# Half the feed-forward steps: 86 of 264 weight pieces by seven block products in place of eight

## The chip, the cores and the metric

The kernel runs on one core of one Trainium2 chip, as one launch. The metric is the device time of that core in microseconds, the median of the runs. The core has a matrix engine (TensorE, PE in the rows, with its weight loads as PEld), a vector engine (VectorE, DVE), an activation engine (ScalarE, ACT), GpSimd (POOL) and a queue engine that issues the transfers (SyncE, SP). Each takes its instructions in a fixed order.

## The reference

One layer of a hybrid decoder over 256 tokens of width 2048, in float32. What matters here are its two half steps, which hold some three fifths of the weights:

```python
D_MODEL = 2048
SEQ = 256
D_FF = 5632

def swiglu(x, w_gu, w_down):
    g, u = jnp.split(x @ w_gu, 2, axis=-1)
    return (jax.nn.silu(g) * u) @ w_down
...
        h = h + 0.5 * swiglu(rmsnorm(h, ffn1_norm[i]), ffn1_w_gu[i], ffn1_w_down[i])
...
        h = h + 0.5 * swiglu(rmsnorm(h, ffn2_norm[i]), ffn2_w_gu[i], ffn2_w_down[i])
    return rmsnorm(h, final_norm)
```

Between the half steps stand one input projection with a gating group and a state-space scan, one output projection, and cross attention into 256 memory tokens.

## The kernel before

All weights stream through the core once. The unit of work is a **piece**: 256 rows of a weight matrix (two blocks of 128, `KP`) by 1024 columns (two halves of 512, `j`). For the gate-and-up projection the two halves are the gate columns and the matching up columns of one column group `c` of 512; there are 11 groups of 8 pieces in a half step (a *column* below). For the down projection they are two neighbouring groups of output columns; there, a pass over the hidden pieces is made for output columns 0 and 1 and another for 2 and 3. The hidden width is taken in two parts, groups 0 to 5 and 6 to 10, each followed by its two down passes. Both half steps together have 2 x 11 x 8 = 176 gate-and-up pieces and 88 down pieces, 264.

Products are made to float32 accuracy from two reduced-precision parts of each operand. `split` (L139) takes a raw piece from the `wraw` buffers and makes, for each block of 128 rows, a rounded high part on ScalarE (`whi`, L148) and the remainder on VectorE (`wlo`, L149). `to_operand` (L229) does the same for the tokens: four transposes by TensorE into one PSUM bank (L72), then high and low halves of the operand. In `proj_tok` (L161) each pair of a token block `t` (two of 128) and a row block `k` multiplies into two PSUM banks, one for each half of the columns, by six matmuls of 512 columns (L180 to L185): high by high, high by low and low by high for each half. A piece is therefore 24 matmuls. TensorE's order is the program's order; for ScalarE and VectorE a planner fixes the order ahead of time, so that each of them waits at its head even where something behind is ready.

After the last piece of a column `evac` (L305) makes the hidden values from PSUM: Silu on ScalarE (L307) and one product on VectorE (L308) for each token block. `operand_later` (L249) puts their transposes off by one `step` (L77), that is, behind the first piece of the next column; they are read out by L236 and L237. In a down pass `evac` of `add_proj` (L286) adds 0.5 times the result to the stream `h` (L291). `finish` (L758) makes the final norm; in the last pass the last two pieces are ordered by token block (`apart` 2), so that block 0 is ready early.

PSUM has eight banks: six in the pool `mm` for products, two in `tp` for everything else (`side`, L90). SBUF holds three raw pieces (`wraw`), four halves of high and of low parts (`wsp`) and 13 slots of 8 KB a partition (`big`) for operands. At the start `x` and the first three weight pieces are loaded in turns (L319 to L324), and the operands of blocks 1 to 3 of `x` are made after pieces 1, 3 and 5 (L336).

## Time and profile before

| | us |
|---|---|
| median of 3 runs | 2575.32 (2575.3 to 2578.29) |
| the profiled execution, whole | 2575.8 |
| its span from the first to the last instruction | 2573.9 |
| TensorE matmuls, busy | 2536.2 |
| VectorE, busy | 1376.7 |
| ScalarE, busy | 1160.0 |

Times in rows are microseconds from the start of the span unless they are marked ns. A row of a group gives the line, engine, operation, output and inputs, shapes and count, then the busy time of the group and the mean of one; after the second bar stands the idle time of the engine right before them and what ended it. In a row in order of time the first number is the start and the second the length; a bracket gives the idle time before it and its releaser. Matmul records overlap: a matmul's record is longer than the distance to the next one's start.

### The profile page before, as it was taken

How to read it: one execution, taken by the hardware profiler on the slowest of the kernel's cores; microseconds unless marked ns; L12 is line 12 of the kernel's file. 1: busy time of each engine (PE TensorE's matmuls, PEld its weight loads, DVE VectorE, ACT ScalarE, POOL GpSimd, SP SyncE). 2: the span in 40 equal slices, each digit the busy share in tenths (PEclk: the TensorE clock that was granted, in tenths of full speed). 3: DMA queues.
4: the chain of work that ended last, by engine and by line, in shares of the span. 5: the costliest groups of instructions: out<-in, count | busy, mean ns of one | idle time of the engine just before them, and what ended most of it. 6: DMA issues, size and time to landing. Idle time of an engine off the chain costs nothing.

```text
span 2573.9 us, 31721 instructions
## 1 busy us (share of the span) xinstructions
PE 2536.2 (99%) x12990; PEld 2166.1 (84%) x12990; DVE 1376.7 (53%) x1445; ACT 1160.0 (45%) x1389; POOL 20.3 (1%) x44
## 2 busy tenths in 40 slices
PE   7999999999999999999999999999999999999998
PEld 6888888888889988788888999988888888888886
DVE  4545444544557667655555555555554454445454
ACT  5444433444445455535544544444444443344443
POOL 0000000000000000000000000000000000000000
PEclk9999999999999999999999999999999999999999
DMA  6555555555654555545655655555555556656564
GB/s 222 190 191 185 195 190 191 192 188 188 196 168 165 181 173 191 190 153 183 194 186 189 213 181 164 164 179 168 191 185 193 184 192 195 193 186 199 188 196 135
DMA packets 190368, 476.74 MB, mean 185 GB/s; under 512 B 12576, under 2 KB 12736, under 8 KB 189456
## 3 DMA queue, kind: packets, MB, share of 16 engines
q1 hardware_dynamic: 188400, 465.87, 55.7%
q0 software_dynamic: 1680, 8.73, 1.0%
q8 instruction: 101, 1.65, 0.3%
q14 instruction: 43, 0.35, 0.0%
q10 hardware_dynamic: 144, 0.13, 0.0%
HBM read 472.57 MB, written 2.13 MB: 184 GB/s over the span
## 4 chain that ended last, share of the span: by engine, by line
PE 97%; DMA 1%; DVE 1%; issue 0%; ACT 0%; SPq 0%; DVEq 0%; POOLq 0%; POOL 0%; ACTq 0%
PE acc L69 93%; PE tpose L72 2%; PE yp L69 1%; PE logits L69 0%; PE o L69 0%; DMA raw<-in_w_gu 0%; DMA dec<-cum_rows 0%; PE mixed L69 0%; ACT whi L148 0%; DVE cacc L376 0%; DVE wlo L149 0%; PE dt L69 0%; PE st L69 0%; PE scores L69 0%; PE yo L69 0%
## 5 line engine op out<-in xcount | busy, mean ns | idle before, releaser
L149 DVE TENSOR_TENSOR wlo<-raw,whi 128x1024 fp32r<-128x1024 f32 x880 | 1076.3, 1225 | 1073.8 <-ACT whi L148 1068.6
L148 ACT CAST whi<-raw 128x1024 fp32r<-128x1024 f32 x880 | 925.0, 1052 | 1229.3 <-PE acc L69 1209.6
L69 PE MATMUL acc<-whi,xt_ffn 128*128 128x512 f32 x2816 | 880.1, 391 | 8.7 <-ACT whi L148 8.7
L69 PEld LDWEIGHTS acc<-whi,xt_ffn 128*128 128x128 f32 x2816 | 529.3, 188 | 118.5 <-ACT whi L148 9.1
L69 PE MATMUL acc<-wlo,xt_ffn 128*128 128x512 f32 x1408 | 548.9, 390 | 0.5 <-DVE wlo L149 0.5
L69 PE MATMUL acc<-whi,hid 128*128 128x512 f32 x1408 | 436.8, 390 | 0.0
L69 PEld LDWEIGHTS acc<-wlo,xt_ffn 128*128 128x128 f32 x1408 | 264.8, 188 | 54.8 <-DVE wlo L149 1.0
L69 PEld LDWEIGHTS acc<-whi,hid 128*128 128x128 f32 x1408 | 264.3, 188 | 54.7
L69 PE MATMUL acc<-wlo,hid 128*128 128x512 f32 x704 | 274.0, 389 | 0.0
L69 PE MATMUL acc<-whi,xt_mix 128*128 128x512 f32 x768 | 242.5, 393 | 0.0
L69 PE MATMUL acc<-xt_mix,whi 128*128 128x256 f32 x1024 | 187.3, 285 | 0.0
L69 PEld LDWEIGHTS acc<-whi,xt_mix 128*128 128x128 f32 x768 | 144.2, 188 | 30.3 <-ACT whi L148 0.5
L69 PEld LDWEIGHTS acc<-xt_mix,whi 128*128 128x128 f32 x1024 | 160.9, 193 | 0.3
L69 PEld LDWEIGHTS acc<-wlo,hid 128*128 128x128 f32 x704 | 132.2, 188 | 27.3
L69 PE MATMUL acc<-wlo,xt_mix 128*128 128x512 f32 x384 | 149.7, 390 | 0.0
L69 PE MATMUL acc<-xt_mix,wlo 128*128 128x256 f32 x512 | 145.5, 284 | 0.0
L69 PEld LDWEIGHTS acc<-xt_mix,wlo 128*128 128x128 f32 x512 | 98.9, 193 | 0.0
L69 PE MATMUL acc<-memt,whi 128*128 128x256 f32 x512 | 92.9, 284 | 0.0
L69 PE MATMUL acc<-xt_xa,whi 128*128 128x256 f32 x512 | 92.9, 284 | 0.0
L69 PEld LDWEIGHTS acc<-wlo,xt_mix 128*128 128x128 f32 x384 | 72.1, 188 | 15.4 <-issue 0.7
L69 PE MATMUL acc<-whi,at 128*128 128x512 f32 x256 | 80.3, 391 | 0.0
L69 PEld LDWEIGHTS acc<-xt_xa,whi 128*128 128x128 f32 x512 | 79.8, 192 | 0.1
(211 smaller groups left out, 1904.9 us busy)
## 6 DMA issues: line engine op xcount, KB each, us to landing
raw<-in_w_gu SPq DMA_DIRECT2D x346, 512.0 KB, 4.5
raw<-in_w_dn SPq DMA_DIRECT2D x88, 1024.0 KB, 5.6
raw<-in_w_in SPq DMA_DIRECT2D x80, 1024.0 KB, 5.1
raw<-in_w_out SPq DMA_DIRECT2D x32, 1024.0 KB, 5.8
raw<-in_w_kv SPq DMA_DIRECT2D x32, 1024.0 KB, 5.4
raw<-in_w_q SPq DMA_DIRECT2D x16, 1024.0 KB, 5.2
raw<-in_w_o SPq DMA_DIRECT2D x16, 1024.0 KB, 5.9
dec<-cum_rows POOLq DMA_DIRECT2D x4, 1024.0 KB, 5.9
```

The costliest lines, as they stand in the source:

```text
L69: return pe(nc.tensor.matmul(out, lhsT=lhsT, rhs=rhs, start=start, stop=stop))
L72: return pe(nc.tensor.transpose(out=out, in_=in_, identity=identity))
L148: nc.scalar.copy(out=hi, in_=raw[:, k])
L149: nc.vector.tensor_tensor(out=lo, in0=raw[:, k], in1=hi.bitcast(F32), op=ALU.subtract)
```

## The change

Seen as two by two blocks, a piece multiplies four token blocks A(t, k) with four weight blocks B(k, j) into four outputs C(t, j), in eight block products. The change makes 86 of the 264 pieces of the two half steps (marked S) by Strassen's method in Winograd's form, with seven products of sums; the other 178 (C) stay as they were.

- For an S piece `split_sums` makes four sums of the raw weight blocks in float32 on VectorE, then high and low parts of three raw blocks and of the four sums. `Pieces.add` makes three plain forms and four sums of the token blocks, and their parts. `proj_sum` multiplies seven times, three matmuls each.
- Four products (m1, m6, m5, m7) collect in four banks of their own over all S pieces of a column or pass, the three others and the fourth output block (c11) with the C pieces. After the last S piece `mid` combines the four on VectorE. After the last piece `evac` adds the result to the other four. All eight banks are now one pool, and between the first and the last S piece no put-off job runs (`shut`).
- A column has its kinds in `GU_KINDS` (three of eight S), a down pass in `DN_KINDS` (two of ten or three of twelve). The hidden width is split after five groups in place of six. In the first column the pieces come in the order `FIRST`.
- High and low parts are made for a whole piece by one instruction, with three and two buffers; the sums and their parts have one buffer each. `big` has 12 slots in place of 13. Small tensors of the middle stages move into the buffers of the sums, and the memory kept for descriptors shrinks to 4096.
- The last pass no longer joins its last two pieces.

```diff
     wraw = ctx.enter_context(tc.tile_pool(name="wraw", bufs=3))
-    wsp = ctx.enter_context(tc.tile_pool(name="wsp", bufs=4))
-    big = ctx.enter_context(tc.tile_pool(name="big", bufs=13))
+    whigh = ctx.enter_context(tc.tile_pool(name="whigh", bufs=3))
+    wlow = ctx.enter_context(tc.tile_pool(name="wlow", bufs=2))
+    wsum = ctx.enter_context(tc.tile_pool(name="wsum", bufs=1))
+    wshigh = ctx.enter_context(tc.tile_pool(name="wshigh", bufs=1))
+    wslow = ctx.enter_context(tc.tile_pool(name="wslow", bufs=1))
+    big = ctx.enter_context(tc.tile_pool(name="big", bufs=12))
...
-    mm = ctx.enter_context(tc.tile_pool(name="mm", bufs=6, space=PSUM))
-    tp = ctx.enter_context(tc.tile_pool(name="tp", bufs=2, space=PSUM))
+    mm = ctx.enter_context(tc.tile_pool(name="mm", bufs=8, space=PSUM))
...
-    def step(to=None):
+    def step(shut=False):
...
         for job in sorted(put_off, key=lambda j: j[:2]):
-            if job[0] <= steps[0] or to == "end":
+            if job[0] <= steps[0] and not shut:
                 put_off.remove(job)
                 job[2]()
...
     def side(name):
-        return tp.tile([P, NC], F32, name=name, tag="tp")
...
+    PLAIN = {(0, 0): 0, (0, 1): 1, (1, 0): 2, (1, 1): 3}
+    FOR_SUMS = {(0, 0): 0, (1, 0): 1, (1, 1): 2, (0, 1): 3}
+
+    def load(w, r0, cs, at, fine=False):
+        raw = wraw.tile([P, 2 * KP, NC], F32, name="raw")
+        rows = w[r0:r0 + KP * P, :]
+        if at is PLAIN and cs[1] == cs[0] + NC:
...
+        for j, c in enumerate(cs):
+            b, e = at[0, j], at[1, j]
+            src = rows[:, c:c + NC]
+            if e > b and not fine:
+                nc.sync.dma_start(out=raw[:, b:e + 1:e - b, :], in_=src.rearrange("(k p) n -> p k n", p=P))
+                continue
+            for k, x in enumerate((b, e)):
+                nc.sync.dma_start(out=raw[:, x, :], in_=src[k * P:(k + 1) * P, :])
         return raw
...
-    def split(raw, behind=()):
-
-        parts = []
-        for k in range(KP):
-            hi = wsp.tile([P, 2, NC], F32R, name="whi")
-            lo = wsp.tile([P, 2, NC], F32R, name="wlo")
-            with ExitStack() as order:
-                for ins in behind:
-                    order.enter_context(tc.issue_after(ins))
-                nc.scalar.copy(out=hi, in_=raw[:, k])
-                nc.vector.tensor_tensor(out=lo, in0=raw[:, k], in1=hi.bitcast(F32), op=ALU.subtract)
-            parts.append((hi, lo))
-        return parts
+    def high(pool, x, n):
+        t = pool.tile([P, 2 * KP, NC], F32R, name="hi")
+        nc.scalar.copy(out=t[:, :n], in_=x[:, :n])
+        return t
+
+    def low(pool, x, hi, n):
+        t = pool.tile([P, 2 * KP, NC], F32R, name="lo")
+        nc.vector.tensor_tensor(out=t[:, :n], in0=x[:, :n], in1=hi[:, :n].bitcast(F32), op=ALU.subtract)
+        return t
...
+    def split(raw):
+        hi = high(whigh, raw, 2 * KP)
+        return hi, low(wlow, raw, hi, 2 * KP)
...
+    def split_sums(raw):
+        t = wsum.tile([P, 4, NC], F32, name="sum")
+        nc.vector.tensor_tensor(out=t[:, 0:2], in0=raw[:, 0:3:2], in1=raw[:, 3:4].broadcast_to([P, 2, NC]), op=ALU.add)
+        nc.vector.tensor_tensor(out=t[:, 2], in0=t[:, 0], in1=raw[:, 2], op=ALU.add)
+        nc.vector.tensor_tensor(out=t[:, 3], in0=t[:, 2], in1=raw[:, 1], op=ALU.add)
+        hi = high(whigh, raw, 3)
+        lo = low(wlow, raw, hi, 3)
+        thi = high(wshigh, t, 4)
+        tlo = low(wslow, t, thi, 4)
+        return [(hi[:, i], lo[:, i]) for i in range(3)] + [(thi[:, i], tlo[:, i]) for i in range(4)]
...
-    def proj_tok(w, r0, xts, cs, evac, kts=D // P, apart=1):
...
-            parts = {i: load_split(w, r0 + i * KP * P, cs) for i in pieces}
-            order = [(t, i, k) for i in pieces for k in range(KP) for t in range(NT)]
-            if ng in (0, len(groups) - 1):
+        for i in range(n):
+            hi, lo = split(load(w, r0 + i * KP * P, cs, PLAIN))
...
+    SOWN = {"m2": (2, 1), "m3": (6, 2), "m4": (1, 6)}
+    SHARED = {"m1": (0, 0), "m6": (5, 5), "m5": (4, 3), "m7": (3, 4)}
+    HOME = {(0, 0): "m2", (0, 1): "m3", (1, 0): "m4", (1, 1): "c11"}
...
+    def proj_sum(w, r0, xps, kinds, cs, mid, evac, order=None, hooks=()):
+        n = len(kinds)
+        order = list(range(n)) if order is None else order
+        s_at = [m for m, i in enumerate(order) if kinds[i] == "S"]
+        c_at = [m for m, i in enumerate(order) if kinds[i] == "C"]
+        banks = {}
...
+        def product(name, pairs, stop):
+            start = name not in banks
+            if start:
+                banks[name] = side("acc")
+            seq = [x for ah, al, bh, bl in pairs for x in ((ah, bh), (ah, bl), (al, bh))]
+            for m, (a, b) in enumerate(seq):
+                matmul(banks[name], a, b, start=start and m == 0, stop=stop and m == len(seq) - 1)
+
+        for m, i in enumerate(order):
+            end = m == n - 1
+            key = (id(w), r0, i, cs)
+            sums = kinds[i] == "S"
+            raw = ready.pop(key) if key in ready else load(w, r0 + i * KP * P, cs, FOR_SUMS if sums else PLAIN)
+            if sums:
+                parts = split_sums(raw)
+                x = xps[i]
+                names = ["m1", "m2", "m3", "m6", "m5", "m7", "m4"]
+                if m == s_at[-1]:
+                    names = ["m1", "m6", "m5", "m7", "m2", "m3", "m4"]
+                for name in names:
+                    f, b = {**SOWN, **SHARED}[name]
+                    product(name, [(x[:, 0, f], x[:, 1, f], *parts[b])],
+                            m == s_at[-1] if name in SHARED else end)
+                    if m == s_at[-1] and name == "m7":
+                        mid([banks[k] for k in ("m1", "m6", "m5", "m7")])
+            else:
+                hi, lo = split(raw)
+                x = xps[i]
+                for (t, j), name in HOME.items():
+                    ts, tl = slice(t * P, (t + 1) * P), slice(S + t * P, S + (t + 1) * P)
+                    product(name, [(x[:, k, ts], x[:, k, tl], hi[:, 2 * k + j], lo[:, 2 * k + j]) for k in range(KP)],
+                            m == (c_at[-1] if name == "c11" else n - 1))
+                    if end and j == 1:
+                        evac(t, [banks[HOME[t, 0]], banks[name]])
+            step(shut=s_at[0] - 1 < m < s_at[-1])
...
+        def add(self, srcs, q, c0):
+
+            kind = self.kinds[len(self)]
+            if kind == "C":
+                if self.half is None:
+                    two = slot([P, 2, KP, 2 * S], F32R, self.name)
+                    dst, self.half = two[:, 0], two[:, 1]
+                else:
+                    dst, self.half = self.half, None
+                self.append(dst)
+                return to_operand(srcs, dst, 0, c0, q)
+            dst = slot([P, 2, 7, P], F32R, self.name + "s")
+            self.append(dst)
+
+            ps = side("tpose").rearrange("p (f s) -> p f s", f=4)
+            for f, (t, k) in enumerate(((1, 0), (0, 0), (1, 1), (0, 1))):
+                transpose(out=ps[:, f], in_=srcs[t][:, (q + k) * P:(q + k + 1) * P], identity=ident)
+            a = half_k(F32, "forms").rearrange("p (f s) -> p f s", f=4)
+            if c0 is None:
+                nc.scalar.copy(out=a, in_=ps)
+            else:
+                for k in range(2):
+                    nc.scalar.activation(a[:, 2 * k:2 * k + 2], ps[:, 2 * k:2 * k + 2], AF.Copy,
+                                         scale=col[:, c0 + q + k:c0 + q + k + 1])
+
+            b = half_k(F32, "forms").rearrange("p (f s) -> p f s", f=4)
+            nc.vector.tensor_tensor(out=b[:, 0:2], in0=a[:, 0:1].broadcast_to([P, 2, P]), in1=a[:, 1:3], op=ALU.subtract)
+            nc.vector.tensor_tensor(out=b[:, 2], in0=a[:, 1], in1=b[:, 1], op=ALU.subtract)
+            nc.vector.tensor_tensor(out=b[:, 3], in0=a[:, 3], in1=b[:, 2], op=ALU.subtract)
+            for x, f0, f1 in ((a[:, 1:4], 0, 3), (b, 3, 7)):
+                hi = nc.scalar.copy(out=dst[:, 0, f0:f1], in_=x)
+                lo = nc.vector.tensor_tensor(out=dst[:, 1, f0:f1], in0=x, in1=dst[:, 0, f0:f1].bitcast(F32),
+                                             op=ALU.subtract)
+            return hi.ins, lo.ins
+
...
+    GU_KINDS = "CSCSCSCC"
+
+    DN_KINDS = {5: ("CCSCCSCCCC", None), 6: ("CCCCSCCSCCSC", [0, 1, 2, 3, 4, 5, 6, 7, 8, 10, 9, 11])}
...
+    def ffn(nrm, w_gu, w_dn, done, order=None):
+        for c_from, c_to in ((0, 5), (5, 11)):
+            kinds, turn = DN_KINDS[c_to - c_from]
+            hts = Pieces(kinds, "hid")
             for c in range(c_from, c_to):
+                m = {}
                 gs = []
 
+                def mid(banks):
+                    m1, m6, m5, m7 = banks
+                    for name in ("m1", "z", "y", "y2"):
+                        m[name] = half_k(F32, "part")
+                    nc.scalar.copy(out=m["m1"], in_=m1)
+                    total(m["z"], m6, m["m1"], ALU.subtract)
+                    total(m["y"], m5, m["z"])
+                    total(m["z"], m7, m["z"])
+                    total(m["y2"], m7, m["y"])
+
                 def evac(t, ps):
-                    g = half_k(F32, "gate")
-                    nc.scalar.activation(g, ps[0], AF.Silu, scale=nrm.rstd[:, t:t + 1])
-                    nc.vector.scalar_tensor_tensor(out=g, in0=ps[1], scalar=nrm.rstd[:, t:t + 1],
-                                                   in1=g, op0=ALU.mult, op1=ALU.mult)
+                    g, u = (m["z"], m["y2"]) if t else (m["m1"], m["y"])
+                    total(g, ps[0], g, ALU.subtract if t else ALU.add)
+                    nc.scalar.activation(g, g, AF.Silu, scale=nrm.rstd[:, t:t + 1])
+                    total(u, ps[1], u)
+                    nc.vector.scalar_tensor_tensor(out=g, in0=u, scalar=nrm.rstd[:, t:t + 1], in1=g,
+                                                   op0=ALU.mult, op1=ALU.mult)
                     gs.append(g)
...
-                proj_tok(w_gu, 0, nrm.xts, (c * NC, DFF + c * NC), evac, kts=D // P)
-                operand_later(gs, hts, "hid")
-            add_proj(w_dn, c_from * NC, hts, 0.5, done if c_to == 11 else None, kts=(c_to - c_from) * KG,
-                     **(kw if c_to == 11 else {}))
...
+                proj_sum(w_gu, 0, nrm.xts, GU_KINDS, (c * NC, DFF + c * NC), mid, evac, order if c == 0 else None)
+                hts.later(gs)
+            for n in (0, 2):
+                def mid(banks):
+                    m1, m6, m5, m7 = banks
+                    a, v, y = (half_k(F32, "part") for _ in range(3))
+                    nc.scalar.copy(out=a, in_=m1)
+                    total(v, m6, a, ALU.subtract)
+                    axpy(h[n][:, 0, :], 0.5, a)
+                    total(y, m5, v)
+                    total(v, m7, v)
+                    axpy(h[n + 1][:, 0, :], 0.5, y)
+                    total(y, m7, y)
+                    axpy(h[n][:, 1, :], -0.5, v)
+                    axpy(h[n + 1][:, 1, :], 0.5, y)
...
+                def evac(t, ps):
+                    for j in range(2):
+                        axpy(h[n + j][:, t, :], 0.5, ps[j])
+
+                proj_sum(w_dn, c_from * NC, hts, kinds, (n * NC, (n + 1) * NC), mid, evac, turn)
...
+    FIRST = [0, 2, 4, 1, 6, 3, 5, 7]
     for n in range(4):
         for t in range(NT):
             nc.sync.dma_start(out=h[n][:, t, :], in_=x_v[:, t, n * NC:(n + 1) * NC])
...
+        if n < 3:
+            ready[id(w_gu1), 0, FIRST[n], (0, DFF)] = load(w_gu1, FIRST[n] * KP * P, (0, DFF), PLAIN, fine=True)
...
+    def x_operand(n):
+        for q in (0, 2):
+            n1.xts.add([h[n][:, t, :] for t in range(NT)], q, n1.c0 + n * KG)
...
+        later(lambda n=n: x_operand(n), by=n)
...
-        later(lambda n=n: n1.stats(n), by=4 + n)
+        later(lambda n=n: n1.stats(n), by=3)
...
+    misc = wsum.tile([P, 4, NC], F32, name="sum").rearrange("p a n -> p (a n)")
...
-        scan["states"] = states = slot([P, GROUPS, REP * HD], F32, "states")
+        scan["states"] = states = wslow.tile([P, GROUPS, REP * HD], F32, name="lo")
...
-    ffn(n2, w_gu2, w_dn2, finish, {"apart": 2})
-    step("end")
+    ffn(n2, w_gu2, w_dn2, finish)
...
-    nc = bacc.Bacc("TRN2", target_bir_lowering=False, num_devices=1)
+    nc = bacc.Bacc("TRN2", target_bir_lowering=False, num_devices=1, dynamic_dma_scratch_size=4096)
```

## Rows read from the trace of the kernel before

**Rows 1.** The page's first part: busy time, share of the span and instructions.

```profile
PE 2536.2 (99%) x12990; PEld 2166.1 (84%) x12990; DVE 1376.7 (53%) x1445; ACT 1160.0 (45%) x1389; POOL 20.3 (1%) x44
```

**Rows 2.** The page's chain that ended last, by engine.

```profile
PE 97%; DMA 1%; DVE 1%; issue 0%; ACT 0%; SPq 0%; DVEq 0%; POOLq 0%; POOL 0%; ACTq 0%
```

**Rows 3.** The page's costliest groups: low halves, matmuls, weight loads.

```profile
L149 DVE TENSOR_TENSOR wlo<-raw,whi 128x1024 fp32r<-128x1024 f32 x880 | 1076.3, 1225 | 1073.8 <-ACT whi L148 1068.6
L69 PE MATMUL acc<-whi,xt_ffn 128*128 128x512 f32 x2816 | 880.1, 391 | 8.7 <-ACT whi L148 8.7
L69 PEld LDWEIGHTS acc<-whi,xt_ffn 128*128 128x128 f32 x2816 | 529.3, 188 | 118.5 <-ACT whi L148 9.1
```

**Rows 4.** Order of time, TensorE, in a down pass (start, length).

```profile
302.04 0.39 PE L69 MATMUL acc<-wlo,hid 128*128 128x512 f32 x1
...
304.76 0.39 PE L69 MATMUL acc<-wlo,hid 128*128 128x512 f32 x1
```

**Rows 5.** Order of time, ScalarE: the second Silu of two columns in succession.

```profile
64.33 0.69 ACT L307 ACTIVATE gate<-acc,rstd_ffn 128x512 f32<-128x512 f32 x1
...
108.82 0.69 ACT L307 ACTIVATE gate<-acc,rstd_ffn 128x512 f32<-128x512 f32 x1
```

**Rows 6.** Stretches: length, busy time by engine, granted clock, DMA share, GB/s.

```profile
64.33:108.82 44.49, 44.49 (x201) 36.82 (x200) 22.12 (x21) 19.10 (x20) 0.00 (x0) 1.00 0.59 190
930.00:1110.00 180.00, 173.58 (x917) 146.48 (x916) 126.01 (x126) 86.05 (x110) 7.95 (x11) 0.99 0.54 183
1100.00:2561.00 1461.00, 1460.80 (x7399) 1245.91 (x7397) 760.71 (x770) 650.11 (x769) 6.04 (x10) 1.00 0.57 183
```

**Rows 7.** Groups by line and shape, VectorE and ScalarE: prices of single instructions.

```profile
L514 DVE TENSOR_TENSOR dec<-dec,lim 128x2048 f32<-128x2048 f32 x4 | 9.1, 2283 | 0.0
L658 DVE TENSOR_TENSOR qt<-acc,qt 128x512 fp32r<-128x512 f32 x8 | 5.5, 688 | 2.2 <-ACT qt L657 2.2
L308 DVE SCALAR_TENSOR_TENSOR gate<-acc,rstd_ffn,gate 128x512 f32<-128x512 f32 x44 | 32.9, 748 | 21.3 <-ACT gate L307 21.3
L369 DVE TENSOR_TENSOR xin<-acc,rstd_b 128x256 f32<-128x256 f32 x32 | 12.5, 421 | 1.0 <-PE acc L69 0.9
L515 ACT ACTIVATE dec<-dec 128x2048 f32<-128x2048 f32 x4 | 7.7, 1922 | 4.0 <-DVE dec L514 4.0
```

**Rows 8.** Order of time, VectorE: neighbours that don't depend, and a dependent chain.

```profile
65.42 0.74 DVE L308 SCALAR_TENSOR_TENSOR gate<-acc,rstd_ffn,gate 128x512 f32<-128x512 f32 x1
66.08 1.22 DVE L149 TENSOR_TENSOR wlo<-raw,whi 128x1024 fp32r<-128x1024 f32 x1
...
799.64 1.26 DVE L421 SCALAR_TENSOR_TENSOR sp<-sp,sp 128x64 f32<-128x64 f32 x5
```

**Rows 9.** Waits of SP's queue: in total, times, longest.

```profile
SPq L135 <- DVE wlo L149: 768.7, 169, 8.3
```

**Rows 10.** Order of time, SP's queue, at the start.

```profile
12.18 2.37 SPq L321 DMA_DIRECT2D h<-in_x  x4
```

**Rows 11.** Waits of TensorE over the whole span: in total, times, longest.

```profile
PE tpose L72 <- ACT xf L378: 7.0, 4, 1.9
...
PE mixed L69 <- DVE v L604: 2.9, 1, 2.9
```

**Rows 12.** Order of time, VectorE, around that wait.

```profile
1076.53 2.29 DVE L513 TENSOR_TENSOR dec<-dec,cum 128x2048 f32<-128x2048 f32 x1 [1.17 <-DMA dec<-cum_rows]
1078.73 0.68 DVE L604 TENSOR_TENSOR v<-mixed,wn 128x512 f32<-128x512 f32 x1
```

**Rows 13.** Order of time, ScalarE and TensorE at the start.

```profile
13.55 0.63 ACT L217 ACTIVATE junk<-h 128x512 f32<-128x512 f32 x1 [4.93 <-DMA h<-in_x]
15.62 0.79 PE L69 MATMUL acc<-whi,xt_ffn 128*128 128x512 f32 x1 [8.66 <-ACT whi L148]
```

**Rows 14.** Order of time, VectorE, the first token block at the end.

```profile
2555.61 1.29 DVE L291 SCALAR_TENSOR_TENSOR h<-acc,h 128x512 f32<-128x512 f32 x2 [2.90 <-PE acc L69]
2557.09 0.69 DVE L764 TENSOR_TENSOR h<-h,fw 128x512 f32<-128x512 f32 x1 [0.19 <-ACT junk L217]
```

More of the change, by code (lines that the diff above doesn't have):

```diff
@@ L206, in proj_feat @@
                     o = ps[c // 2][:, c % 2, :]
-                    matmul(o, hi[:, cs], xt[:, :S], start=first and c % 2 == 0, stop=False)
-                    matmul(o, hi[:, cs], xt[:, S:])
-                    matmul(o, lo[:, cs], xt[:, :S], start=False, stop=last and c % 2 == 1)
+                    matmul(o, hi[:, k, cs], xt[:, :S], start=first and c % 2 == 0)
+                    matmul(o, hi[:, k, cs], xt[:, S:])
+                    matmul(o, lo[:, k, cs], xt[:, :S], stop=last and c % 2 == 1)
             step()
@@ L360, in hybrid_layer @@
     PAD = CONV - 1
-    xin = [const.tile([P, PAD + S], F32, name=f"xin{i}") for i in range(3)]
+    xin = [misc2[:, i * 260:i * 260 + PAD + S] for i in range(3)]
     for xi in xin:
```

124 lines of the change are left out of this document (57 added, 67 removed).

## The prediction

> **What bounds the kernel now.** I read the head of the page first: the matmul row is busy 99% of the span at the full granted clock, VectorE 53%, ScalarE 45% [rows 1], and the chain that ended last runs 97% through matmuls [rows 2]. A busy matmul row proves little by itself, because records overlap (390 ns each in [rows 3], but they start closer together). So I went to the order of time. In the steady stretch twelve 512-column matmuls start between 302.04 and 304.76 us (groups of 1, 3, 1, 1, 1, 3, 1, 1 rows): 2.72 us, so one takes **0.2267 us** [rows 4]. A piece of 24 takes 5.44 us. One gate-and-up column (eight pieces, then eight transposes) repeats every 108.82 - 64.33 = 44.49 us [rows 5]: 192 x 0.2267 = 43.52, and 0.97 for the transposes. Nothing is left over, and from 1100 to 2561 us TensorE idles 0.2 us in 1461 [rows 6]. TensorE's column time is the bound. In such a column VectorE works 22.12 us and ScalarE 19.10 [rows 6], so half of VectorE is free, and that half is what the change spends.
>
> **What it removes.** A summed piece does seven block products of three matmuls, 21, where a plain piece does 24. Summed pieces: three in each of 22 columns (66), and 2 x (2 + 3) in each of the two down projections (20), so 86. 86 x 3 = 258 matmuls x 0.2267 = **58.5 us**, of which 22 x 9 x 0.2267 = 44.9 lie in the columns and 13.6 in the down passes. Transposes keep their number: a summed operand turns the same four blocks. A column is then (5 x 24 + 3 x 21) x 0.2267 + 0.97 = **42.46 us** of TensorE.
> [...]
>
> **What it adds to VectorE, per column.** Prices are from [rows 7]: 2.283 us for two inputs of 2048, 0.688 for 512, 0.748 for 512 with a scalar column, 0.421 for 256; and 1.225 for 1024 [rows 3].
> - A plain piece: one low half of 2048, 2.283. Five: 11.42.
> - A summed piece: sums of 1024, 512 and 512 (1.225 + 2 x 0.688), low half of 1536 (between 1.225 and 2.283, so 1.754), low half of the sums 2.283: 6.64. Three: 19.92.
> - Early combinations (`mid`): 4 x 0.688 = 2.75. Late ones: 4 x 0.688 + 2 x 0.748 = 4.25.
> - Operands of the down projection: plain 0.688; summed 0.421 + 2 x 0.29 (128 wide, between the 0.25 of 64 in [rows 8] and 0.421) + 0.556 (384, between 256 and 512) + 0.688 = 2.25. 17 plain and 5 summed over 11 columns: 2.09.
>
> Sum: **40.43 us of VectorE against 42.46 of TensorE**, 95%, where it was 50%. Independent neighbours start early: 65.42 + 0.74 ends at 66.16, yet the next starts at 66.08, so about 0.08 is shared, while five 64-wide ones that depend on each other take 1.26 us, 0.25 each, one after the other [rows 8]. With 34 instructions a column, up to 2.7 us comes off: 37.7 to 40.4, or 89 to 95%.
> [...]
>
> ScalarE: 5 x 1.92 for plain high halves, at most 3 x (1.92 + 1.92) for summed ones (1.92 for 2048 [rows 7]), and a copy, two Silu and the operand copies, some six instructions of 512 at 1.92 / 3: 25 us, 59%. It doesn't bind. The bytes of a column stay, so the rate goes from 190 GB/s at a DMA share of 0.59 [rows 6] to 190 x 44.49 / 42.46 = 199 at 0.62. On SP's queue stands one issue more per summed piece (three transfers for two), in front of the next load; SP waited 769 us for VectorE to free buffers in those loads [rows 9], so I cost it at nothing. Without that cover it is 2.37 / 4 = 0.59 us an issue [rows 10], 51 us for 86, one fifteenth of that wait.
>
> **New waits.** (1) Sums and their two halves have one buffer each. The low half of the next sums stands in VectorE's queue until TensorE has left the summed piece before; behind it stand the plain low halves and the combinations that free banks. Between two summed pieces lies a plain one of 5.44 us, and what must fit there is 1.754 + 2.283 = 4.04: it fits. (2) The transposes stand in TensorE's order after the first piece of the next column and need both halves of the late combinations. From the end of the token half 0, 2.72 us before the column's end, to the transposes is 8.16 us; 4.25 + the low half of the next sums' raw blocks (1.754) = 6.0 are due there, plus at most one 2.283 already begun. It fits with little to spare. (3) All eight banks are open inside the summed stretch, so deferred jobs are shut out there, and product five of the first summed piece waits until a transpose's bank is read.
>
> **What the stalls cost.** The trace of before has no stretch with VectorE at 90%. The nearest below is the column at 50%, stall 0. Above it, at 930 to 1110 us, VectorE is at 126 of 180 us [rows 6], 2.28 us instructions among it, and there TensorE waited once 2.9 us [rows 11] for a product that stood behind one of 2.29 [rows 12]: 2.9 / 180 x 42.46 = 0.68 us per column if that recurs at this rate. No row excludes more: with one such wait in each column it is 2.9. I take **0.6 x 22 = 13 us**, near the 0.68, with 0 and 2.9 a column as ends; below 0 it can't be, since the columns of before have no idle time to give.
>
> Other places. **Down passes**: VectorE has 3 x 6.64 + 9 x 2.283 + 8 x 0.69 + 4 x 0.69 = 48.7 us for 63.2 of TensorE; 2 us, between 0 and 8 over eight passes. **Start**: the first matmul waits until 15.62 because ScalarE stood at a statistic of the second block of x until 13.55 [rows 13]. With the load of x's second block ahead of the second weight piece this may shrink by 4 us; but the operands of all four blocks now fall before the fourth piece: on VectorE three low halves 6.85, operands 5 x 2 x 0.48 + 3 x 2.25 = 11.5, the first summed piece 6.64, so 25 us beside three pieces and three rounds of transposes, 19, and two summed pieces are neighbours there, so the second waits for its high and low sums (1.92 + 2.283 less one product of 0.68, 3.5 us). I take +3, between -4 and +8. **Middle**: low halves in lumps of 2.28 instead of 1.22 lengthen waits like the 7.0 us on `xf` [rows 11] by up to 8 us; eight shared banks instead of six and two may save up to the 6 us of TensorE's idle time there (180 - 173.58 [rows 6]); I take 0. **End**: the first token half is done 2.72 us before the last matmul instead of 5.44. Its work (two updates, squares, a product: 2.2 us from 2555.61 to 2557.78 [rows 14]) still ends about when the second half's begins; +0.5, between 0 and 2.7.
>
> **Sum**, against the profiled 2575.8 us (2573.9 span and 1.9 around it; 0.5 above the median 2575.3): 2575.8 - 58.5 + 13 + 2 + 3 + 0 + 0.5 = **2535.8 us**, say 2536.
>
> **Rivals.**
> - *A, forecast, 0.66*: VectorE keeps up with small stalls. Own range 2509 (all stalls at the lower end, 2575.8 - 58.5 - 4, and a part of the middle's 6) to 2556 (1.5 us a column).
> - *B, 0.18*: VectorE becomes the bound in the columns. Its 40.43 plus some 4 us a column in which its head waits for a buffer that TensorE holds give about 44.5, the old period. Then only the down passes pay: 2575.8 - 13.6 = 2562. For it: 95%, and single buffers. Against it: a period's demands fit, counted above.
> - *C, slower, 0.10*: the fixed order of VectorE's queue puts a 2.28 us low half ahead of a combination that the transposes or a bank wait for, as in [rows 12], 2.9 us each time. Once per column: 22 x 2.9 = 63.8, so 2575.8 - 58.5 + 63.8 + 5.5 = 2587. It decides from (58.5 - 5.5) / 2.9 = 18 times on. Against it: the columns of before show no such wait in 22 repeats, but with VectorE half free.
> - *D, 0.04*: a removed matmul gives back less than its slot, because weight loads set the pace: 258 x 0.188 [rows 3] = 48.5, so 2546. Against it: loads end before the next start and the spacing is even. [...]
> - *E, 0.02*: the change doesn't do what it says, with fewer than 86 pieces on the short path or longer slots from other addresses: no change, 2576.
>
> **Chances.** About 0.2% (5 us) is what a measurement can tell from no change, so faster is below 2570. A and D whole, four fifths of B: 0.66 + 0.04 + 0.15 = 0.85. Same: the rest of B and E, 0.05. Slower: C, 0.10. The range runs from A's lower end, 2509, over most of B, to 2568: outside lie C, E and the ends of A and B, 0.2.
>
> **What would show it.** Matmuls of 512 columns fewer by 258 at the same 0.2267 us; gate-and-up columns 42.5 to 43.5 us apart with VectorE near 95%; TensorE idle mostly for releases by VectorE, after the first piece of a column. Columns at 44.5 with VectorE without a gap mean B. A wait of 2 to 3 us in each column, with a low half running while a combination is ready, means C. It is wrong from the ground up if the spacing changes, or if the idle time is ScalarE's or the DMA's.

## The result, and the profile after

| | before | after |
|---|---|---|
| median (lowest to highest of 4 runs), us | 2576.81 (2575.3 to 2578.4) | 2545.31 (2543.63 to 2546.85) |
| profiled execution, whole / its span, us | 2575.8 / 2573.9 | 2544.5 / 2542.8 |
| matmuls of 128x128 by 512 columns in the trace | 9040 | 8782 |

The ratio is 0.9878 (95% interval 0.986 to 0.9895). The change saves 31 us; the forecast of 2536 had it save 40. Both the sign and the range held; the sum is 8.7 us under the profiled 2544.5.

The first part of the page after, beside [rows 1]; then the chain, beside [rows 2]:

```profile
PE 2491.5 (98%) x12732; PEld 2126.1 (84%) x12732; DVE 1822.0 (72%) x1644; ACT 1233.8 (49%) x1100; POOL 21.3 (1%) x44
...
PE 90%; DVE 6%; ACT 2%; issue 1%; DMA 1%; SPq 0%; ACTq 0%; DVEq 0%; POOL 0%
```

258 matmuls are gone (12990 - 12732, all of them of 512 columns), VectorE works 445 us more, and the chain still runs 90% through TensorE. The spacing is the old one, as the order of time of TensorE in a down pass shows, beside [rows 4]:

```profile
289.87 0.62 PE L73 MATMUL acc<-hi,hid 128*128 128x512 f32 x2
...
292.59 0.62 PE L73 MATMUL acc<-hi,hid 128*128 128x512 f32 x2
```

Between these two starts lie twelve matmuls: 2.72 / 12 = 0.2267 us. The columns, by the second Silu of three in succession, beside [rows 5]:

```profile
398.92 0.71 ACT L436 ACTIVATE part<-part,rstd_ffn 128x512 f32<-128x512 f32 x1
...
441.29 0.72 ACT L436 ACTIVATE part<-part,rstd_ffn 128x512 f32<-128x512 f32 x1
...
483.67 0.71 ACT L436 ACTIVATE part<-part,rstd_ffn 128x512 f32<-128x512 f32 x1
```

42.37 and 42.38 us, where 42.46 was forecast. Stretches of after, beside [rows 6] (length, then busy time of PE, PEld, DVE, ACT and POOL with their instructions, then granted clock, DMA share, GB/s): one column, most of the second half step, and the first 100 us.

```profile
441.29:483.67 42.38, 42.38 (x193) 35.18 (x192) 37.45 (x33) 22.37 (x18) 0.00 (x0) 1.00 0.62 199
2100.00:2530.00 430.00, 429.53 (x1920) 355.78 (x1918) 358.86 (x305) 213.73 (x154) 2.20 (x4) 1.00 0.60 193
0.00:100.00 100.00, 78.90 (x320) 61.26 (x321) 70.57 (x77) 53.98 (x65) 2.58 (x11) 0.95 0.57 186
```

TensorE is without a gap in a steady column, VectorE busy 88% beside it. In 430 us of the second half step TensorE idles 0.5. The first 100 us are another matter: 21 idle, at a mean clock of 0.95. TensorE's waits after, beside [rows 11] (in total, times, longest):

```profile
PE tpose L76 <- ACT xf L534: 10.4, 4, 3.8
PE acc L73 <- DVE xp_ffn L300: 6.9, 5, 2.3
PE acc L73 <- ACT xp_ffn L299: 6.8, 2, 5.3
PE acc L73 <- DVE lo L148: 5.9, 10, 1.8
```

For the comparisons below I took, for each TensorE instruction, the distance to the next one's start less the median distance of its shape; what is over is TensorE's lost time, waits and slowed matmuls alike. By place, in us (the start is from TensorE's first instruction, at some 4.3, to 100; the second half step's start its first 60; the tail what follows the last matmul's start). The last column has the time in which the trace has the granted clock at 0.5, in the start, the middle and the second start, in whole us:

| kernel | start | rest of half step 1 | middle | second start | rest of half step 2 | tail | half clock |
|---|---|---|---|---|---|---|---|
| before | 13.0 | 0.1 | 22.2 | 0.1 | 0.0 | 13.1 | 0, 3, 0 |
| after | 27.8 | 2.3 | 27.1 | 5.5 | 0.9 | 12.3 | 10, 14, 3 |
| plain | 15.0 | -0.7 | 28.7 | 0.0 | -0.8 | 11.8 | 0, 17, 0 |
| gu_only | 28.1 | 0.0 | 27.4 | 5.3 | 0.4 | 12.2 | 10, 14, 3 |
| dn_only | 14.4 | -0.7 | 28.7 | 0.0 | -0.8 | 11.7 | 0, 14, 0 |
| order2 | 21.5 | 1.2 | 24.8 | 5.5 | 1.0 | 12.4 | 7, 7, 3 |
| no_low_sums | 19.2 | -0.3 | 26.2 | 3.9 | -0.1 | 12.2 | 0, 10, 0 |
| halves | 23.3 | 2.1 | 25.5 | 6.2 | 1.0 | 12.2 | 7, 14, 3 |
| best | 25.7 | 1.2 | 24.0 | 5.3 | 1.0 | 12.6 | 10, 10, 3 |
| order_mid | 21.5 | 1.3 | 25.2 | 4.0 | 1.9 | 12.4 | 3, 14, 0 |

From before to after the losses grow by 75.9 - 48.5 = 27.4 us; with the 58.5 of removed matmuls that is the 31.1 by which the spans differ.

Waits are about half of the 27.4. Added up over the whole span, those of TensorE grow from 25.2 to 39.1 us; 10.4 of the 13.9 are for VectorE, 3.6 for ScalarE. The rest is mostly TensorE's granted clock: the time at 0.5, the tail aside, grows from 3 to 27 us, and as a matmul takes 0.427 us in place of 0.227 there (last section), 24 us more of it lose at most 11 us, by my estimate. Each kernel was profiled once, and the same wait is followed by slowed matmuls in one trace and not in another (order2 and order_mid below). So a difference of 2 us at one place of the table says something of the order of work only if the waits differ too.

### The profile page after: what moved, and what is told of

The parts are those of the page before. It is cut to its first block, busy times and chain, and to the rows that moved or that the text cites. A ratio compares the mean times of both kernels' runs of the same rounds, so it can differ in the third digit from the quotient of the medians.

```text
span 2542.8 us, 31168 instructions
## 1 busy us (share of the span) xinstructions
PE 2491.5 (98%) x12732; PEld 2126.1 (84%) x12732; DVE 1822.0 (72%) x1644; ACT 1233.8 (49%) x1100; POOL 21.3 (1%) x44
## 4 chain that ended last, share of the span: by engine, by line
PE 90%; DVE 6%; ACT 2%; issue 1%; DMA 1%; SPq 0%; ACTq 0%; DVEq 0%; POOL 0%
PE acc L73 86%; DVE lo L148 3%; PE tpose L76 2%; ACT hi L143 1%; PE yp L73 1%; DMA raw<-in_w_gu 0%; DVE cacc L532 0%; PE logits L73 0%; PE o L73 0%; DVE sum L159 0%; DVE sum L161 0%; PE mixed L73 0%; DVE sum L160 0%; DVE hids L361 0%; PE dt L73 0%
## 5 line engine op out<-in xcount | busy, mean ns | idle before, releaser
L148 DVE TENSOR_TENSOR lo<-raw,hi 128x2048 fp32r<-128x2048 f32 (+1 forms) x440 | 959.5, 2183 | 443.9 <-PE acc L73 360.0
L143 ACT CAST hi<-raw 128x2048 fp32r<-128x2048 f32 (+1 forms) x440 | 805.1, 1830 | 950.5 <-PE acc L73 802.9
L73 PE MATMUL acc<-hi,xp_ffn 128*128 128x512 f32 x1760 | 558.5, 392 | 10.2 <-ACT xp_ffn L299 6.8
L73 PEld LDWEIGHTS acc<-hi,xp_ffn 128*128 128x128 f32 x1760 | 332.5, 189 | 82.9 <-ACT xp_ffn L299 8.7
L73 PE MATMUL acc<-lo,xp_ffn 128*128 128x512 f32 x880 | 344.4, 391 | 1.2 <-DVE lo L148 1.2
L73 PE MATMUL acc<-hi,hid 128*128 128x512 f32 x1088 | 340.4, 390 | 0.0
L148 DVE TENSOR_TENSOR lo<-sum,hi 128x2048 fp32r<-128x2048 f32 x86 | 196.8, 2289 | 117.3 <-ACT hi L143 117.3
L73 PE MATMUL acc<-hi,xt_mix 128*128 128x512 f32 x768 | 244.4, 395 | 0.0
L73 PEld LDWEIGHTS acc<-hi,hid 128*128 128x128 f32 x1088 | 204.2, 188 | 42.3
L73 PE MATMUL acc<-lo,hid 128*128 128x512 f32 x544 | 211.7, 389 | 0.0
L73 PE MATMUL acc<-hi,xp_ffn1s 128*128 128x512 f32 x462 | 150.4, 394 | 3.4 <-ACT hi L143 1.8
L73 PEld LDWEIGHTS acc<-lo,hid 128*128 128x128 f32 x544 | 102.2, 188 | 20.9
```

What stands on the lines that cost most here:

```text
L73: return pe(nc.tensor.matmul(out, lhsT=lhsT, rhs=rhs, start=start, stop=stop))
L143: nc.scalar.copy(out=t[:, :n], in_=x[:, :n])
L148: nc.vector.tensor_tensor(out=t[:, :n], in0=x[:, :n], in1=hi[:, :n].bitcast(F32), op=ALU.subtract)
```

## The experiments

Theory P: the removed matmuls pay in full, and what is lost is lost at the two starts and in the middle. Rival Q: the rebuilt kernel costs something of its own everywhere, or (Q2) the down passes lose what they save. Rival R: the starts' losses are the amount of VectorE's work, whatever its order. Diffs are against the kernel after.

### All pieces plain: plain

```diff
-    GU_KINDS = "CSCSCSCC"
+    GU_KINDS = "CCCCCCCC"
-    DN_KINDS = {5: ("CCSCCSCCCC", None), 6: ("CCCCSCCSCCSC", [...])}
+    DN_KINDS = {5: ("CCCCCCCCCC", None), 6: ("CCCCCCCCCCCC", None)}
```

Where a column has no summed piece, here and in dn_only, `evac` is that of before, without combinations.

> All 264 pieces plain, the rest of the change kept (whole-piece parts, one bank pool, split after five groups, new first order). Theory P (the seven products pay in full, what is lost is lost at the two starts and in the middle stages): the start without summed operands idles 10 to 15 us (before 13), the middle loses its 5 us more, the gate-and-up columns stand at 44.49 us: 2575 to 2583 us. Rival Q (the rebuilding itself costs, whole-piece parts and the bank pool, whatever the sums do): 2595 us or more, with columns above 44.5.

Measured: 2579.81 us (2579.23 to 2582.29), 1.001 of before (1.0 to 1.0019). All else that the change rebuilds (whole-piece halves, the split of the hidden width, eight shared banks, order at the start) costs 2.2 us in all, with 0 to 5 by the interval. Q falls. The middle's 28.7 us, 6.5 above before's, are already there without one summed piece.

### Summed pieces in the columns alone, and in the down passes alone: gu_only, dn_only

gu_only leaves `GU_KINDS` as in after and makes `DN_KINDS` plain; dn_only the reverse.

> Summed pieces in the gate-and-up columns alone, down passes plain. P: the 20 summed down pieces pay their 13.6 us in full, so the changed kernel's 2545.3 + 13.6 = 2559 us, columns at 42.4. Rival Q2 (the down passes lose as much to their late and early combinations as they save): 2545 to 2550.

> Summed pieces in the down passes alone. P: 13.6 us below the all-plain version, whatever that shows, about 2563 to 2569, columns at 44.49 and both starts as in the all-plain version. Q2: the same as all plain.

Measured: gu_only 2555.3 us (2553.71 to 2556.05), 24.5 below plain; dn_only 2568.4 us (2566.72 to 2569.74), 11.4 below plain. Together 35.9, and the kernel with both stands 34.5 below plain, so they hardly disturb each other. The down passes pay 11.4 of their 60 x 0.2267 = 13.6 us beside plain columns and 10.0 beside summed ones (gu_only less after; I had expected gu_only at 2559). That is most of it, so Q2 falls; beside summed columns the table has 2.8 us more lost in the steady parts of after than of gu_only. The columns pay 24.5 of their 198 x 0.2267 = 44.9, and the table says where the other 20 went: 28.1 - 15.0 = 13.1 at the start, 5.3 at the second start, some 2 in the steady parts. So the losses at both starts belong to the summed gate-and-up pieces.

### The order of the first columns: order2

```diff
-    FIRST = [0, 2, 4, 1, 6, 3, 5, 7]
+    FIRST = [0, 2, 1, 4, 3, 6, 5, 7]
...
-        later(lambda n=n: x_operand(n), by=n)
+        later(lambda n=n: x_operand(n), by=min(n, 2))
...
-        later(lambda n=n: n1.stats(n), by=3)
+        later(lambda n=n: n1.stats(n), by=2)
...
-    ffn(n2, w_gu2, w_dn2, finish)
+    ffn(n2, w_gu2, w_dn2, finish, FIRST)
```

> The changed kernel with the first column of both half steps in the order 0, 2, 1, 4, 3, 6, 5, 7: two plain pieces first, no two summed pieces as neighbours; the statistics one piece earlier. P: the 4.1 us wait of the second neighbour for the high and low part of its sums goes, with the stretch of half clock behind it (about 1.4 us); in the second half step the wait of 2.5 us for a bank, the 1.1 before it and 1.4 us of half clock go: 2532 to 2538 us. Rival R (the idle time of a start is VectorE's work in any order): within 2 us of 2545.3, the waits only move.

What it is to remove, in TensorE's, VectorE's and ScalarE's order of time after: pieces 3 and 5, both summed, are neighbours there.

```profile
61.73 0.39 PE L73 MATMUL acc<-hi,xp_ffn1s 128*128 128x512 f32 x1
63.95 0.49 PE L73 MATMUL acc<-hi,xp_ffn1s 128*128 128x512 f32 x1 [1.83 <-ACT hi L143]
66.28 0.80 PE L73 MATMUL acc<-lo,xp_ffn1s 128*128 128x512 f32 x1 [1.83 <-DVE lo L148]
...
61.21 0.68 DVE L161 TENSOR_TENSOR sum<-sum,raw 128x512 f32<-128x512 f32 x1
63.93 2.29 DVE L148 TENSOR_TENSOR lo<-sum,hi 128x2048 fp32r<-128x2048 f32 x1 [2.04 <-ACT hi L143]
...
62.00 1.90 ACT L143 CAST hi<-sum 128x2048 fp32r<-128x2048 f32 x1 [1.28 <-DVE sum L161]
```

The sums end at 61.89, their high half takes ScalarE until 63.90, their low half VectorE until 66.22, and TensorE waits for each in turn, 1.83 + 1.83 us.

Measured: 2536.52 us (2535.25 to 2537.61), 0.9838 (0.9824 to 0.9853), 8.8 below after. By its total P is right, by its places half: the start falls by 6.3, and this double wait is gone from it (in exchange a wait of 3.4 us for a transpose's bank has come), but the second start stays at 5.5, its wait moved to low halves later in the stage. There R had it right. Of the start's 6.3 us, 4.0 are waits (20.9 to 16.9 us in the first 100) and the rest slowed matmuls, 7 us at half clock in place of 10. 2.3 us are the middle's, where the order doesn't reach: its waits are the same to 0.1 us, and only the time at half clock is shorter, 7 us in place of 14.

### Less work for VectorE in the same order: no_low_sums

```diff
-        tlo = low(wslow, t, thi, 4)
+        tlo = thi
```

> Leaves out the low parts of the summed weights (86 subtractions of 128x2048 at 2.29 us on VectorE; the matmuls stay and read the high part twice), so the output is another one. VectorE's work falls by 86 x 2.29 = 197 us (7.5 to 7.8 us in each gate-and-up column), TensorE's not at all. Theory P (the columns are paced by TensorE; what is lost at the starts is the order of the work, ending on ScalarE's casts and on waits for transposes): the steady column stays at 42.4 us, the start's idle time falls only by the wait for the sums' low half and what hangs on it, from 27.8 to 22-26 us, the second start's from 5.4 to 4-5.4: 2538 to 2543. Theory R (the starts' losses are VectorE's work, in whatever order): start 15 to 20 us, second start 0 to 2 us: 2529 to 2536. If the columns were still VectorE's, each would get shorter, by up to 22 x 0.5: under 2528.

Measured: 2532.47 us (2529.69 to 2533.04), 0.9822 (0.9805 to 0.9838). Total and start (19.2) are as R said; the columns stay at 41.9 to 42.8 us, though VectorE has 197 us less to do, so they are TensorE's, as P said. The second start measures 3.9, P's edge, but its waits are those of after (2.4 and 1.0 us, there 2.3 and 1.0): only the 3 us at half clock are gone, so less work changed no wait there. In the first start the waits fall from 20.9 to 16.4 us in the first 100, and the 10 us at half clock go. The profiled execution is also the shortest of the four. So at the first start the order (6.3 us) and the work (8.6) each take away some 4 us of waits, and the rest goes with less time at half clock, 7 and 0 us in place of 10. The two remedies overlap, since both end the wait for the sums' low half, and no run has both. Some 6 us remain that this run does not take away.

### A dose of VectorE work: dose and dose2

```diff
                 hi, lo = split(raw)
+                for _ in range(dose[c_at.index(m)]):
+                    nc.vector.tensor_tensor(out=dump, in0=..., in1=..., op=ALU.add)
```

dose reads a constant, dose2 the high half of the piece.

> Adds VectorE work that nobody waits for behind the low halves of plain pieces: 3 additions of 128x512 (0.68 us each, 2.0 us) in each of the first half step's 11 columns, 10 (6.8 us) in each of the second's. VectorE's busy time in a column is 39.4 to 41.7 us of 42.4 after the change. Theory A (VectorE lies under a ceiling and only its sum counts): the first half step's columns stay within 42.4 to 43.7 us, the second's become VectorE's at 46 to 48.5 us: +0 to 14 and +40 to 67 us, 2585 to 2620. Theory C (the order of VectorE's queue decides: whatever stands ahead of a late combination costs): 1 to 2 us more already in each column of the first half step, +11 to 22 there: 2605 to 2640. Theory B' (the columns have been VectorE's all along): +2.0 in each of the first 11, +6.8 in each of the second: +97 us, 2642.

> The dose once more, tied to its place: additions of 128x512 (0.68 us) on VectorE that read the high half of the piece they stand behind, so that they can't be put forward, in the gate-and-up columns of the second half step alone: 3 in each of its columns 0 to 3 (2.1 us), 6 in columns 4 to 7 (4.1 us), 10 in columns 8 to 10 (6.9 us). In the first dose's columns VectorE's durations reached 1.03 to 1.06 us per us of time. Theory A (VectorE has room up to its sum): 39.6 to 41.6 us of its own plus the dose, over 1.045: columns 0 to 3 stay at 42.4 to 43.3 us, 4 to 7 at 42.4 to 44 us, 8 to 10 at 44.3 to 46 us: 2548 to 2560. Theory C (each piece of work ahead of a late combination costs): 1 to 2 us in columns 0 to 3 already, 2 to 4 in 4 to 7, 4 to 7 in 8 to 10: 2569 to 2590.

dose measured 2576.12 us (2573.25 to 2577.28), below every number expected, since the planner did not leave the additions where I had put them: as they depend on nothing, it put all 143 between 7.5 and 484 us, those for the second half step too. So it tells nothing of the two doses, but something of VectorE's room. Four columns in after, the same four in dose with 48 additions, and the stretch with the down passes in dose with 53 additions, 36.4 us:

```profile
78.18:248.25 170.07, 169.19 (x761) 139.45 (x760) 150.42 (x133) 90.25 (x68) 0.00 (x0) 1.00 0.61 195
...
83.69:273.30 189.61, 178.66 (x775) 144.89 (x774) 183.89 (x186) 93.30 (x70) 0.00 (x0) 0.97 0.56 180
...
273.30:422.56 149.26, 149.19 (x663) 123.34 (x662) 147.81 (x148) 67.40 (x43) 0.00 (x0) 1.00 0.60 197
```

In the columns VectorE goes from 150.4 busy of 170.1 us to 183.9 of 189.6, 97%: nearly the state of rival B. But of the 19.5 us that they take longer, 3.2 are fourteen matmuls more in the stretch, 9.0 are three waits for low halves, up to 3.5 us each, and 1.9 are waits for `hid`; 10 us lie at half clock. In the down stretch VectorE is 99% busy, and hardly anything is lost: 149.3 us without one wait of TensorE, where after takes 150.7 with eight matmuls, 1.8 us, more. So in this one stretch 36.4 us of work, freely placed, cost 0.4 us, with VectorE all but full.

dose2 measured 2585.48 us (2584.44 to 2587.07), 1.0031 (1.002 to 1.0041), 40 above after: theory C's range by its total, but not spread as C had it: of the second half step's columns 3 and 5 don't grow, 2 and 6 grow by 5 us. From 1870 us on TensorE waits 24 us, 1 in after, and 27 us lie at half clock, none in after. Four columns and five columns of the second half step in after, the same in dose2 with 14 and with 40 additions (9.6 and 27.4 us):

```profile
1873.89:2042.00 168.11, 167.64 (x756) 138.75 (x755) 148.49 (x133) 88.30 (x68) 0.00 (x0) 1.00 0.61 197
2192.67:2402.97 210.30, 209.83 (x946) 173.78 (x945) 185.96 (x164) 110.86 (x83) 0.00 (x0) 1.00 0.61 197
...
1877.75:2058.49 180.74, 172.68 (x756) 141.62 (x755) 157.50 (x147) 88.34 (x67) 0.00 (x0) 0.97 0.58 183
2207.97:2445.43 237.46, 221.11 (x951) 179.63 (x950) 211.60 (x205) 112.53 (x85) 0.00 (x0) 0.96 0.54 176
```

12.6 us longer for 9.6 us of work, 27.2 (with five matmuls, 1.1 us, more) for 27.4, and VectorE is busy only 87 and 89%: not its sum, but its queue and the slowed matmuls behind the waits. The first of the long waits in dose2's order of time, VectorE and then TensorE:

```profile
1943.99 0.69 DVE L163 TENSOR_TENSOR sum<-sum,raw 128x512 f32<-128x512 f32 x1
1946.63 2.29 DVE L150 TENSOR_TENSOR lo<-raw,hi 128x2048 fp32r<-128x2048 f32 x1 [1.95 <-PE acc L73]
1948.84 2.28 DVE L150 TENSOR_TENSOR lo<-sum,hi 128x2048 fp32r<-128x2048 f32 x1
...
1951.18 0.79 PE L73 MATMUL acc<-lo,xp_ffn2s 128*128 128x512 f32 x1 [3.51 <-DVE lo L150]
```

VectorE idles for 1.95 us with the low half of a plain piece at its head, whose buffer TensorE frees only at about 1946.6. Behind it stands the low half of the sums, which TensorE needs next. The same place of the same column in after has the two in the other order, and TensorE does not wait:

```profile
1937.43 0.69 DVE L161 TENSOR_TENSOR sum<-sum,raw 128x512 f32<-128x512 f32 x1
1940.17 2.29 DVE L148 TENSOR_TENSOR lo<-sum,hi 128x2048 fp32r<-128x2048 f32 x1 [2.05 <-ACT hi L143]
1942.38 2.28 DVE L148 TENSOR_TENSOR lo<-raw,hi 128x2048 fp32r<-128x2048 f32 x1
```

Two additions stand earlier in that column of dose2, at 1927 and 1934 us. So with 1.4 us more of work in the column the planner has turned two entries round, and that costs a wait of 3.5 us. Theory A, right for after, does not hold one step beyond it.

### Smaller parts in the middle and at the starts: halves, best, order_mid

```diff
+        for a in range(0, n, 2):
+            b = min(n, a + 2)
+            nc.scalar.copy(out=hi[:, a:b], in_=raw[:, a:b])
+            nc.vector.tensor_tensor(out=lo[:, a:b], in0=raw[:, a:b], in1=hi[:, a:b].bitcast(F32), op=ALU.subtract)
```

halves does this in the first column of each half step and in those projections of the middle that run through `proj_feat` (the projections through `proj_tok` keep parts of 128x2048); best adds the first half step's order of order2; order_mid is order2 with the parts in the middle alone.

> Casts and low halves of 128x2048 and 128x1536 in parts of 128x1024 (and 128x512), as the kernel before had them: in the middle and in the first column of each half step; 0.2 us more on each engine for a piece. Theory H (part of what the middle and the starts lose comes from short work standing behind a cast of 1.9 us or a low half of 2.3 us): the waits for xf go back from 2.3 to 4.0 us to about 2.0, the middle's idle time from 27.1 to 21-24 us, the starts fall by 1 to 4 us together: 2536 to 2542. Theory R: only the sum of the work counts, the middle and the starts stay or grow by a little: 2544 to 2549.

> The parts of the run with halves, and the first half step's first column in the order 0, 2, 1, 4, 3, 6, 5, 7 so that a plain piece stands between any two summed ones. If the two remedies add up (H): 2545 - 6.3 (start, by order) - 3 to 5 (middle) - 0 to 3 (starts, by halves) = 2531 to 2536, below every kernel so far. If the halves only help where the order had left a wait: 2534 to 2538. R: 2538 to 2542.

> The order 0, 2, 1, 4, 3, 6, 5, 7 in the first columns of both half steps, and casts and low halves in parts of 128x1024 in the middle alone, not in the first columns (where the run with both had taken 4 us more at the start than the order alone). If the two add up: the start's idle time 21.5 us, the middle's 22.5 to 24 us (no wait of 0.4 us for a low half, 0.7 in place of 1.8 us for dt; the four waits for xf stay at 2.3 to 4.0): 2533 to 2536. If not: 2536 to 2539.

Measured: halves 2536.73 us (2535.74 to 2538.81), 0.9838; best 2537.46 (2536.34 to 2538.81), 0.984; order_mid 2535.04 (2534.75 to 2536.03), 0.9834 (0.9819 to 0.9849). halves is 8.6 below after, as H had it (its profiled execution, the longest of the four, 5.7), but not by the places that H named. The waits for `xf` did not shrink:

```profile
PE tpose L76 <- ACT xf L542: 10.8, 4, 3.8
```

That is 10.8 us, where after has 10.4 and before 7.0 [rows 11]. Only small waits of the middle went (for `dt` 1.6 to 0.5, and three for low halves, 0.7 together), and the middle's loss fell by 1.6 us; 4.5 came from the start. The remedies don't add: best's start is 25.7, worse than with either alone, because a double wait comes back from 76 us on, now in the second column: its first summed piece waits 1.5 us for the high half of its sums and then 2.8 for the low half. order_mid has order2's start. The waits of its middle are 1.4 us shorter (11.3 in place of 12.7), but with 14 us at half clock in place of 7 that middle is no shorter; at the second start its waits are order2's, and it is 1.5 us shorter without the half clock. So its total lies where I had put remedies that add up, but the places don't show that they do. Its 2535.04 is the lowest of the complete kernels, but its runs overlap with those of order2 and halves.

What makes the waits for `xf` longer than before's stays open in part. plain has them at 10.4 too, so it is not the summed pieces. The four are 1.85, 1.85, 1.85 and 1.49 us before; 2.21, 2.17, 2.17 and 3.84 after. halves does not settle whether the width of the parts does it. Ahead of the fourth, which has 2.35 of the 3.4 us, the parts are still whole (VectorE, then TensorE, in halves):

```profile
948.42 2.29 DVE L148 TENSOR_TENSOR lo<-raw,hi 128x2048 fp32r<-128x2048 f32 x1
950.63 2.19 DVE L540 SCALAR_TENSOR_TENSOR cacc<-hi,col,cacc 128x256 f32<-128x256 f32 x5
...
952.49 0.55 PE L76 MATMUL tpose<-ident,xf 128*128 128x128 f32 x3 [3.83 <-ACT xf L542]
```

The steps of `cacc`, from which `xf` is made, stand behind that low half. Ahead of each of the other three, two halved casts stand right behind each other on ScalarE, 1.99 us together, so that `xf` waits as long as for a whole one of 1.90.

## Why the prediction was right, and which terms were off

**The frame held.** 258 matmuls fewer at 0.2267 us, as counted: rivals D and E are out. A steady column is 42.37 us against 42.46, and no_low_sums shows that VectorE doesn't set it. Its work in a column came to 39.4 us by the lengths of its 33 records and 37.45 by the time in which any ran, just under my 37.7 to 40.4 and 88% where I had looked for 95: the overlap, 1.9 us over 33 records or 0.06 us each, is nearly the 0.08 us of [rows 8].

**Rival B** did not come. The dose bounds the room that I had only guessed: by my estimate four columns have 170.1 x 0.97 - 150.4 = 14.6 us before VectorE is full, 3.6 a column. That holds for its sum alone; in dose2 9.6 us in four columns cost 12.6 already.

**The columns' and down passes' stalls, 13 + 2, were too high.** They measure 2.3 + 0.9 - 0.1 = 3.1 us in all. The step that failed is the transfer of the 2.9 us wait at 1077 us, at a rate per time, from a stage of another kind. In the steady parts TensorE waits five times, 2.2 us in all, for low halves, and never more than 0.5. Of the fourteen columns that neither begin a half step nor touch a down pass nine take 42.37 us, from one's first matmul to the next one's, and five 43.0 to 43.5. VectorE's order differs among them, but columns with the same order have the same length. Why nearly every order fits is not shown; dose2 shows that the worry behind it was sound, and its price as well (from 1870 us on TensorE waits there nine times for low halves, 23.0 us, 2.6 each); after stays just clear of it.

**The start, +3, was mis-sized: it cost 14.8, outside its own -4 to +8.** Three of its parts I had. The first matmul comes at 12.24 us in place of 15.62, 3.4 of the 4 forecast; the neighbours' wait is 3.66, forecast 3.5; VectorE does have more to do than fits. What I set against the 25 us of VectorE work was a sum of three pieces' time, not the order. In that order low halves of weights stand ahead of the low part of the token operand that the piece at hand needs. VectorE, then TensorE:

```profile
29.82 1.76 DVE L148 TENSOR_TENSOR lo<-raw,hi 128x1536 fp32r<-128x1536 f32 x1 [1.01 <-PE acc L73]
31.50 2.28 DVE L148 TENSOR_TENSOR lo<-sum,hi 128x2048 fp32r<-128x2048 f32 x1
33.70 0.48 DVE L300 SCALAR_TENSOR_TENSOR xp_ffn<-tpose,col,xp_ffn 128x256 fp32r<-128x256 f32 x1
...
12.24 0.80 PE L73 MATMUL acc<-hi,xp_ffn 128*128 128x512 f32 x1 [5.35 <-ACT xp_ffn L299]
14.19 0.79 PE L73 MATMUL acc<-lo,xp_ffn 128*128 128x512 f32 x1 [1.16 <-DVE lo L148]
...
34.23 1.01 PE L73 MATMUL acc<-hi,xp_ffn 128*128 128x512 f32 x2 [1.12 <-DVE xp_ffn L300]
35.08 0.51 PE L73 MATMUL acc<-lo,xp_ffn 128*128 128x512 f32 x1
36.77 1.22 PE L73 MATMUL acc<-hi,xp_ffn 128*128 128x512 f32 x2 [1.17 <-DVE xp_ffn L300]
```

The matmul at 34.23 multiplies the low part that ends at 34.18. Only one wait of the first start, 1.4 us at 48.92, is for a bank that a transpose's read has still to free. And two of these groups of waits, at 32 to 37 us and at 64 to 66, are followed by slowed matmuls (last section): 10 us at half clock, none in before, which by my estimate, at 0.427 for 0.227, cost at most 5 of the 14.8. No term of mine held them.

**The second half step's start was left out: 5.4 us.** I had costed waits for the first start and stalls for the columns, and took the second start for a column like the others. But there too operands for eight pieces are made while the first of them are multiplied. This is the third of the new waits that the prediction lists, made worse by rival C's mechanism. VectorE and then TensorE after:

```profile
1834.45 1.75 DVE L148 TENSOR_TENSOR lo<-raw,hi 128x1536 fp32r<-128x1536 f32 x1
1836.28 0.69 DVE L361 TENSOR_TENSOR xp_ffn2s<-forms,xp_ffn2s 128x512 fp32r<-128x512 f32 x1
1836.89 0.48 DVE L300 SCALAR_TENSOR_TENSOR xp_ffn<-tpose,col,xp_ffn 128x256 fp32r<-128x256 f32 x1
...
1837.52 0.77 PE L73 MATMUL acc<-hi,xp_ffn2s 128*128 128x512 f32 x1 [2.30 <-DVE xp_ffn L300]
```

Product five of the first summed piece needs the bank that the read at 1836.89 frees, and that read stands behind a low half and an operand: 2.3 us. So C's mechanism is there, at the starts and not in each column.

**The middle**, taken at 0 with -6 to +8, came to +4.9. The wait of 2.9 us for `mixed` did go; `xf` took 3.4 more, as I feared, and whether by the lumps that I blamed stays open. `dt` and low halves took some 2 more, and the waits for `cumt` and `yoff`, 0.9, went, so that waits make up only 1.5 us of the 4.9. Most of the rest is the clock: 14 us at 0.5, 3 in before. **The end**, +0.5, came to -0.8.

Added up: 2535.8 - 11.9 (columns and down passes) + 11.8 (start) + 5.4 (second start) + 4.9 (middle) - 1.3 (end) = 2544.7, against the profiled 2544.5. That the total came so close is in part luck: one term was too high where three were too low, and no term held the clock.

## What to carry to other kernels

When an engine off the path goes from half to nearly full, cost the places where the pipeline fills one by one; the steady loop may be nearly free (3.1 us lost here) while each start pays for its order (14.8 and 5.4 us), and pays again where the clock falls behind a wait (0.427 us a matmul in place of 0.227). In a fixed order the room left on an engine is not its idle share: one entry that waits for a buffer, ahead of one that somebody needs, can cost more than the work that put it there (3.5 us for 1.4 in dose2). To measure the room, tie the added work to its place by a dependence, or the planner puts it elsewhere (in dose all 143 additions between 7.5 and 484 us).

## What the runs showed of the hardware that I had not expected

Short waits of TensorE were followed in places by matmuls at a granted clock of 0.50. After the waits at 33 and 36 us above, in order of time and as a stretch:

```profile
37.79 0.63 PE L73 MATMUL acc<-lo,xp_ffn 128*128 128x512 f32 x1
...
41.63 0.59 PE L73 MATMUL acc<-lo,xp_ffn 128*128 128x512 f32 x1
...
33.00:42.00 9.00, 6.70 (x16) 4.61 (x16) 6.14 (x13) 6.46 (x20) 0.72 (x1) 0.62 0.32 114
```

Nine matmuls start from 37.79 to 41.63, in 3.84 us, 0.427 each in place of 0.227. The mean granted clock is 0.62 over the stretch shown and 0.50 over those 3.84 us, half of full speed; the nine lose 1.8 us without any wait of their own. The tail aside, the trace after has six stretches at 0.5 behind waits, 27 us in all; before has one, of 3. So these two waits, 2.3 us, and the slowed matmuls behind them cost 4.1. It does not follow each wait: in before the one of 2.9 us at 1077 us [rows 11] was not followed by one. And order2 and order_mid have the same two waits at the second start, 1.0 and 2.5 us, but from 1860 to 1880 us the mean granted clock is 0.91 in the one and 1.00 in the other. What decides it no run here settles.
